# A trunk of retention, dilated attention and gated MLPs on one core: the denominators' selection issued later, a buffer of its own for the transposed values, and part of each layer end's norm work on VectorE

## The chip, the core and the metric

The kernel runs on one core of a Trainium2 chip. The metric is the device time of one execution in microseconds (us). A core has TensorE (PE in the profile, with its weight loads shown as PEld), VectorE (DVE), ScalarE (ACT), GpSimd (POOL) and SyncE (SP), which here only issues the DMAs. Each engine works through its own list of instructions in order and waits for the others on semaphores.

## What is computed

A decoder trunk of two layers over 512 tokens of width 1024, in float32. Layer 0 mixes by retention, layer 1 by dilated attention with three head groups; each is followed by a gated MLP. Every sub-layer is wrapped in two norms:

```
for layer in range(2):
    h = rmsnorm(x, norm_mix_pre[layer])
    m = retention_mixer(h, ...) if layer == 0 else dilated_mixer(h, w_q, w_o, k_sh, v_sh, pos)
    x = x + rmsnorm(m, norm_mix_post[layer])
    f = conv_ffn(rmsnorm(x, norm_ffn_pre[layer]), ...)
    x = x + rmsnorm(f, norm_ffn_post[layer])
    if layer == 0:
        k_sh, v_sh = shared_kv(x, kv_norm, att_w_kv, pos)
```

In the attention the outputs of the three groups of a head are merged by their softmax denominators, which comes to one common maximum and one common sum over the three groups:

```
outs, lses = [], []
for gi, (window, dilation) in enumerate(((128, 1), (512, 4), (2048, 16))):
    o, l = dilated_group_attention(q[:, :, gi], k_sh[:, :, gi], v_sh[:, :, gi], window, dilation)
alpha = softmax(stack(lses), axis=0)
o = einsum('gbsh,gbshd->bshd', alpha, stack(outs))
```

## The kernel before

**Stages.** The program is unrolled: retention (to about 400 us of the profile), first MLP (to 795 us), attention (to 1357 us), second MLP. The 512 tokens are four blocks of 128 rows (`NB` = 4). Each product of two float32 matrices is made of three matmuls (`mm3`, L208 to L210) on a high and a low part of each operand. A weight tile comes by DMA into `raw` (3 buffers), is multiplied by a gain on GpSimd in the attention (L158), and is parted into `whi` on ScalarE (L168) and `wlo` on VectorE (L169).

**Layer ends (`finish`, `prenorm`).** In the last output projection of a sub-layer `contract` goes over the blocks b and, in each, over two halves c of the width. After a half, `after(b, c)` runs: VectorE has added the half to `m` (L271), ScalarE sums its squares (`squares`, L221), and `m` is multiplied with the post-norm's row into `h` (L323). After the second half `rms` makes v_rms (L225) and `rstd` r_rms (L215) on GpSimd; the block's generator then adds to the residual x (L305, VectorE). `prenorm` follows for the next sub-layer: squares of x in two halves, v_rms and r_rms, the scaled rows `h` (L256, or L254 where there is no gain row), four transposes a half on TensorE (L264), and their parting into `hT_hi` (L198) and `hT_lo` (L199). The order on VectorE and GpSimd is as written here (`manual_schedule(engines=ORD)`); TensorE's and ScalarE's order is made by the scheduler that builds the program. In the next MLP `up_first` does its products for tokens 0 to 255 of four weight units, and the last two blocks' steps are called from inside it. At the program's end the last half's product is on VectorE already (`end`).

**Attention (`heads`).** Heads are worked in eight pairs hp. While `heads` does the scores, softmax and output of pair hp, `_weave` interleaves it with a generator `fill` that makes the keys, queries and values of pair hp+1: at each `yield` of `heads` two to four steps of `fill` (three matmuls each) are put in. There the order on TensorE is as written (`manual_schedule(engines={E.PE})`), those of VectorE and ScalarE are the scheduler's, and all are fixed when the program is built.

- `residue_values` makes the values of the dilated groups: the product in `pm`, a copy `vT` to SBUF on ScalarE (L674), and four transposes on TensorE some steps later (L693). `vT` is allocated under the tag `sh`, of which there is one buffer.
- `rotated` makes keys and queries: VectorE shuffles `pm` into `sh` (L714) and multiplies `pm` into `m` (L716, L720), GpSimd multiplies `sh` (L717, L721) and adds it to `m` (L718, L722). `sh` is that same one buffer.
- The scores `sc` (L756) of groups 1 and 2 read four such `m`; VectorE masks them (L760).
- `weights` transposes the probabilities in eight pieces i = 0 to 7 (L846) into `pt`, copied to `pT` by VectorE for even i (L852) and by ScalarE for odd i (L850). `apply` multiplies them with the values into `po` (L866).
- `select` spreads the denominators over a matrix on VectorE (L778) and multiplies with it on TensorE into `pz` (L785); `gather` picks the result up on VectorE (L790, L795), whose inverse (L882, L883) is spread by ScalarE (L885) and transposed (L895) for the last product (L896). `pt`, `pz` and part of `sc` share the PSUM tag `tr`, with two buffers.

Of the kernel before, what the change touches and what calls it, by code (L numbers as in the profile page):

```python
# [17 lines left out]
P = 128  # L18
# [78 lines left out]
def trunk(ctx: ExitStack, tc: tile.TileContext, a, out):  # L97
# [132 lines left out]
    def prenorm(b, gain, both=False):  # L230

        ss = small.tile([P, 2], F32, name="ss", tag="ss")
        for c in range(2):
            if both and c == 1:
                junk = norm.tile([P, 512], F32, name="h", tag="h", bufs=HB)
                nc.vector.tensor_tensor_reduce(
                    out=junk,
                    in0=x[b][:, half(c)],
                    in1=x[b][:, half(c)],
                    scale=1.0 / D,  # L240
                    scalar=0.0,
                    op0=ALU.mult,
                    op1=ALU.add,
                    accum_out=ss[:, c : c + 1],
                )
            else:
                squares(x[b], ss, c)
        r = rms(ss)
        yield
        hs = []  # L250
        for c in range(2):
            h = norm.tile([P, 512], F32, name="h", tag="h", bufs=HB)
            if gain is None:
                nc.vector.tensor_scalar(out=h, in0=x[b][:, half(c)], scalar1=r, scalar2=None, op0=ALU.mult)  # L254
            else:
                nc.vector.scalar_tensor_tensor(  # L256
                    out=h, in0=x[b][:, half(c)], scalar=r, in1=gain[c], op0=ALU.mult, op1=ALU.mult
                )
            hs.append(h)
        yield  # L260
        for c in range(2):
            pt = ps.tile([P, 4, P], F32, name="pt", tag="tr")
            for j in range(4):
                nc.tensor.transpose(out=pt[:, j, :], in_=hs[c][:, blk(j)], identity=ident)  # L264
            split(pt, hi[:, c * 4 : c * 4 + 4, blk(b)], lo[:, c * 4 : c * 4 + 4, blk(b)])
# [27 lines left out]
    def finish(left, w, row, then, ahead=(), tag="po", early=None):  # L293
# [21 lines left out]
        def after(b, c):  # L315
            if c == 0:
                ss[b] = small.tile([P, 2], F32, name="ss", tag="ss")
                steps[b], mg[b] = block(b), []
            mg[b].append(norm.tile([P, 512], F32, name="h", tag="h", bufs=HB))
            squares(m[b], ss[b], c)  # L320
            end = then is None and b == NB - 1
            eng = nc.vector if end and c == 1 else nc.gpsimd
            eng.tensor_mul(out=mg[b][c], in0=m[b][:, half(c)], in1=gain[:, half(c)])  # L323
            if early and ahead:
                t = 2 * b + c
                if t in EP:
                    units.append(parts(raws[len(units)]))
            if c == 0:
                if b >= 1:
                    next(steps[b - 1], None)  # L330
                if b >= 2:
                    next(steps[b - 2], None)
            else:
                rs[b] = rms(ss[b], nc.vector if end else nc.gpsimd)
                if ahead and not early and b == 1:
                    units.append(parts(raws[0]))
                if ahead and not early and b == F4:
                    raws.append(fetch(*ahead[3]))
                if ahead and not early and b == 3:
                    units.append(parts(raws[1]))  # L340
                if b >= 1:
                    next(steps[b - 1], None)
# [270 lines left out]
    def attention(pool, post, then, late, ahead):  # L613
# [11 lines left out]
        with pool as tmp:  # L625
# [37 lines left out]
            def residue_values(hp, g, res):  # L663
# [4 lines left out]
                for k in range(KT):  # L668
                    mm3(pm, [t[:, blk(k)] for t in wu], (hi[:, k, :], lo[:, k, :]), k == 0, k == KT - 1)
                    aged(k)  # L670
                    if k < KT - 1:
                        yield
                vT = tmp.tile([P, SEQ], F32, name="vT", tag="sh", bufs=1)
                nc.scalar.copy(out=in_runs(vT), in_=by_residue(pm))  # L674
                v = rtiles[hp % 2 * 2 + g - 1]
                pending.append([vT, v, 0])
# [54 lines left out]
            def heads(hp, ks, qs, vs, vr, res):  # L731
# [102 lines left out]
                def weights(i, rb):  # L834
# [9 lines left out]
                    for h in range(2):  # L844
                        for n, p in enumerate(src):
                            nc.tensor.transpose(out=pt[:, h, n, :], in_=p[:, h, :], identity=ident)  # L846
                    pT = tmp.tile([P, 2, 2, P], F32, name="pT", tag="pT", bufs=6)
                    n = len(src)
                    if i % 2:
                        nc.scalar.copy(out=pT[:, :, 0:n, :], in_=pt[:, :, 0:n, :])  # L850
# [19 lines left out]
                for i in range(0, 8, 2):  # L870
# [1 line left out]
                        for t in prev:  # L872
                            apply(*t)
                    prev += [(j, order[j], *weights(j, order[j])) for j in (i, i + 1)]
                    if i == 2:
                        pz = select(den[:, 8:16], quarter, sel[:, 0:128])
                    yield
                    yield

                inv = small.tile([P, 8], F32, name="inv", tag="inv", bufs=2)  # L880
                gather(pz, residue, inv)
                nc.vector.tensor_add(out=inv, in0=inv, in1=den[:, 0:8])  # L882
                nc.vector.reciprocal(out=inv, in_=inv)  # L883
                spread = tmp.tile([P, 2, 2, P], F32, name="pT", tag="pT", bufs=6).rearrange("p a b q -> p (a b q)")
                nc.scalar.copy(  # L885
                    out=spread.rearrange("p (c d) -> p c d", d=HD), in_=inv.unsqueeze(2).broadcast_to([P, 8, HD])
                )
# [68 lines left out]
    def pre(row):  # L956
        g = []

        def run(b):
            if not g:  # L960
                t = gain_rows(row)
                g.extend(t[:, half(c)] for c in range(2))
            return prenorm(b, g)

        return run

    mix, ffn_ = a["norm_mix_post"], a["norm_ffn_post"]
    late = retention(pool("ret", "left"), mix[0], pre(a["norm_ffn_pre"][0]), ffn_first(0))
    late = ffn(0, pool("ffn0", "right"), ffn_[0], lambda b: prenorm(b, None), late, att_first())
    late = attention(pool("att", "left"), mix[1], pre(a["norm_ffn_pre"][1]), late, ffn_first(1))  # L970
    ffn(1, pool("ffn1", "right"), ffn_[1], None, late)

# [42 lines left out]
```

## Time and profile before

| | |
|---|---|
| median of 3 runs | 1747.56 us (1743.99 to 1750.20) |
| the profiled execution | 1750.31 us |
| its span, first to last instruction | 1748.5 us |
| mean granted TensorE clock | 0.991 of full speed |
| PE busy in the span | 98% |
| DVE, ACT, POOL busy | 54%, 35%, 23% |
| PE's idle between its own first and last instruction, gaps of over 0.06 us | 28.9 us in 19 places |

The profile has a page of totals, a list of who waited for whom (in total, times, longest), a timeline in which every row has start, duration, engine, line and operation, and in brackets the engine's idle time just before it with what ended that; and busy times by stretch with the clock that the throttle granted. `pz L785 <- DVE pT L852` reads: the instruction of line 785 that writes `pz` stood idle until the instruction of line 852 that writes `pT` on VectorE was done. A matmul's end is modelled, so that a shown idle time of PE starts where the model ends the matmul before.

### The profile page before, as it was taken

To read this page: it belongs to the slowest core of one execution; us is meant where nothing else is said; L and a number is where in the kernel's file an instruction comes from. 1 tells how busy PE (TensorE), PEld (TensorE's weight loads), DVE (VectorE), ACT (ScalarE), POOL (GpSimd) and SP (SyncE) were. 2 spreads that over 40 slices of the span, in tenths; PEclk is the share of its full clock that TensorE was granted. 3 is DMA by queue.
4 is the path that set the end of the run, shared out by engine and by line. 5 is a ranking of instruction groups with operands and counts; after the bars stand their busy time and mean duration, and the time that the engine had idled before them with its cause. 6 is when DMAs were issued, how large, how long until landed. Compare 5 with 4: busy or idle time off the path is not lost.

```text
span 1748.5 us, 21650 instructions
## 1 busy us (share of the span) xinstructions
PE 1709.0 (98%) x8590; PEld 1417.3 (81%) x8590; DVE 939.2 (54%) x1461; ACT 613.3 (35%) x1076; POOL 397.5 (23%) x284
## 2 busy tenths in 40 slices
PE   9999999999999999999899999999999999999998
PEld 6888888887888888878778888878887788888886
DVE  4553545468544544557546556556455754454454
ACT  5232422325442422423144243244245544233241
POOL 1000000005000000046665656566431400000003
PEclk9999999999999999999999999999999999999999
DMA  6422333214332332432222222222221333233231
GB/s 211 125 67 84 91 97 91 85 36 109 121 96 73 121 96 73 133 106 61 85 71 64 85 73 81 68 70 85 69 73 44 87 116 97 83 111 96 84 109 49
DMA packets 202162, 156.10 MB, mean 89 GB/s; under 512 B 4989, under 2 KB 182093, under 8 KB 202062
## 3 DMA queue, kind: packets, MB, share of 16 engines
q1 hardware_dynamic: 202062, 154.73, 28.9%
q8 instruction: 67, 1.10, 0.3%
q14 instruction: 33, 0.27, 0.0%
HBM read 152.62 MB, written 2.10 MB: 88 GB/s over the span
## 4 chain that ended last, share of the span: by engine, by line
PE 89%; DVE 5%; POOL 3%; ACT 1%; issue 1%; DMA 1%; POOLq 0%; SPq 0%; DVEq 0%; ACTq 0%
PE pm L208 20%; PE pm L210 20%; PE pm L209 20%; PE po L208 6%; PE po L209 6%; PE po L210 6%; PE sc L756 2%; DVE wlo L169 2%; PE po L866 2%; PE pt L846 1%; DVE x L305 1%; PE s L450 1%; PE pt L264 1%; DVE h L256 1%; POOL raw L158 1%
## 5 line engine op out<-in xcount | busy, mean ns | idle before, releaser
L208 PE MATMUL pm<-hT_hi,whi 128*128 128x512 f32 (+1 forms) x1424 | 546.3, 384 | 0.0
L209 PE MATMUL pm<-hT_lo,whi 128*128 128x512 f32 (+1 forms) x1424 | 540.0, 379 | 0.3 <-DVE hT_lo L199 0.3
L210 PE MATMUL pm<-hT_hi,wlo 128*128 128x512 f32 (+1 forms) x1424 | 539.7, 379 | 0.0
L169 DVE TENSOR_TENSOR wlo<-raw,whi 128x1024 fp32r<-128x1024 f32 x275 | 377.7, 1378 | 299.9 <-ACT whi L168 296.2
L168 ACT CAST whi<-raw 128x1024 fp32r<-128x1024 f32 x275 | 286.0, 1051 | 650.0 <-PE pm L209 355.3
L208 PEld LDWEIGHTS pm<-hT_hi,whi 128*128 128x128 f32 x1424 | 269.6, 189 | 51.5 <-issue 3.2
L210 PEld LDWEIGHTS pm<-hT_hi,wlo 128*128 128x128 f32 x1424 | 269.3, 189 | 50.1
L209 PEld LDWEIGHTS pm<-hT_lo,whi 128*128 128x128 f32 x1424 | 269.6, 189 | 48.5 <-DVE hT_lo L199 1.2
L158 POOL TENSOR_TENSOR raw<-raw,cols 128x1024 f32<-128x1024 f32 x72 | 140.7, 1957 | 465.8 <-DMA raw<-in_att_w_kv 385.6
L271 DVE TENSOR_TENSOR m<-po,m 128x512 f32<-128x512 f32 x112 | 77.1, 688 | 139.0 <-PE po L210 138.8
L208 PE MATMUL pm<-whi,hT_hi 128*128 128x512 f32 (+1 forms) x384 | 142.2, 370 | 0.0
L323 POOL TENSOR_TENSOR h<-m,gain 128x512 f32<-128x512 f32 x31 | 47.4, 1528 | 407.7 <-DVE m L271 407.2
L208 PE MATMUL po<-whi,ah 128*128 128x512 f32 x352 | 137.9, 392 | 0.0
L209 PE MATMUL po<-wlo,ah 128*128 128x512 f32 x352 | 137.9, 392 | 0.0
L210 PE MATMUL po<-whi,al 128*128 128x512 f32 x352 | 137.8, 391 | 0.0
L210 PE MATMUL pm<-whi,hT_lo 128*128 128x512 f32 (+1 forms) x384 | 136.9, 356 | 0.0
L209 PE MATMUL pm<-wlo,hT_hi 128*128 128x512 f32 (+1 forms) x384 | 136.7, 356 | 0.0
L215 POOL TENSOR_TENSOR r_gn<-v_gn,nhalf 128x1 f32<-128x1 f32 x16 | 8.8, 548 | 357.4 <-DVE v_gn L480 357.4
L208 PEld LDWEIGHTS pm<-whi,hT_hi 128*128 128x128 f32 x384 | 73.0, 190 | 11.5 <-issue 1.0
L209 PEld LDWEIGHTS pm<-wlo,hT_hi 128*128 128x128 f32 x384 | 73.1, 190 | 10.8 <-DVE wlo L169 0.6
L210 PEld LDWEIGHTS pm<-whi,hT_lo 128*128 128x128 f32 x384 | 72.8, 190 | 10.7 <-DVE hT_lo L199 0.3
L208 PEld LDWEIGHTS po<-whi,ah 128*128 128x128 f32 x352 | 66.5, 189 | 14.2 <-DVE m L271 0.4
(137 smaller groups left out, 1959.8 us busy)
## 6 DMA issues: line engine op xcount, KB each, us to landing
raw<-in_ffn_w_up SPq DMA_DIRECT2D x88, 512.0 KB, 3.8
raw<-in_att_w_kv SPq DMA_DIRECT2D x48, 512.0 KB, 4.0
raw<-in_ret_w_in SPq DMA_DIRECT2D x47, 512.0 KB, 3.9
raw<-in_ffn_w_down SPq DMA_DIRECT2D x44, 512.0 KB, 3.2
raw<-in_att_w_q SPq DMA_DIRECT2D x24, 512.0 KB, 3.7
raw<-in_ret_w_out SPq DMA_DIRECT2D x16, 512.0 KB, 3.3
raw<-in_att_w_o SPq DMA_DIRECT2D x8, 512.0 KB, 3.3
x<-in_x SPq DMA_DIRECT2D x3, 512.0 KB, 6.6
```

Of the source, the lines that this page charges most:

```text
L158: nc.gpsimd.tensor_mul(out=dst, in0=dst, in1=gain.unsqueeze(2).broadcast_to(list(src.shape)))
L168: nc.scalar.copy(out=hi, in_=raw)
L169: nc.vector.tensor_sub(out=lo, in0=raw, in1=hi.bitcast(F32))
L208: nc.tensor.matmul(o, lhsT=l[0], rhs=r[0], start=start, stop=False)
L209: nc.tensor.matmul(o, lhsT=l[0], rhs=r[1], start=False, stop=False)
L210: nc.tensor.matmul(o, lhsT=l[1], rhs=r[0], start=False, stop=stop)
L256: nc.vector.scalar_tensor_tensor(out=h, in0=x[b][:, half(c)], scalar=r, in1=gain[c], op0=ALU.mult, op1=ALU.mult)
L264: nc.tensor.transpose(out=pt[:, j, :], in_=hs[c][:, blk(j)], identity=ident)
L271: nc.vector.tensor_add(out=dst, in0=src, in1=dst)
L323: eng.tensor_mul(out=mg[b][c], in0=m[b][:, half(c)], in1=gain[:, half(c)])
L756: nc.tensor.matmul(pm[h][:, i, c], lhsT=q, rhs=k, start=True, stop=True)
L866: nc.tensor.matmul(dst, lhsT=v, rhs=p, start=i == 0 and g == 0, stop=i == 7)
```

## The change

Four things are edited.

1. In `heads`, the `select` of the denominators is issued after the transposes of pieces 4 and 5 and one `yield`, instead of directly behind those of pieces 2 and 3.
2. `vT` has a tag of its own, and so a buffer of its own. `pT` has five buffers instead of six.
3. At every layer end, not only at the program's, the product of the last block's second half with the norm's row is on VectorE instead of GpSimd. (v_rms and r_rms stay on GpSimd except at the program's end.)
4. In the `prenorm` of the last block at the three inner layer ends, the squares of the second half of x are summed by VectorE (L236) instead of ScalarE; its unused product goes to a small tile `junk2` instead of an `h` buffer.

```
@@ prenorm
             if both and c == 1:
-                junk = norm.tile([P, 512], F32, name="h", tag="h", bufs=HB)
+                junk = norm.tile([P, 512], BF16, name="junk2", tag="junk2", bufs=1)
                 nc.vector.tensor_tensor_reduce(
@@ finish, after(b, c)
-            end = then is None and b == NB - 1
+            end = b == NB - 1
             eng = nc.vector if end and c == 1 else nc.gpsimd
             eng.tensor_mul(out=mg[b][c], in0=m[b][:, half(c)], in1=gain[:, half(c)])
...
-                rs[b] = rms(ss[b], nc.vector if end else nc.gpsimd)
+                rs[b] = rms(ss[b], nc.vector if end and then is None else nc.gpsimd)
@@ residue_values
-                vT = tmp.tile([P, SEQ], F32, name="vT", tag="sh", bufs=1)
+                vT = tmp.tile([P, SEQ], F32, name="vT", tag="vT", bufs=1)
@@ heads, weights
-                    pT = tmp.tile([P, 2, 2, P], F32, name="pT", tag="pT", bufs=6)
+                    pT = tmp.tile([P, 2, 2, P], F32, name="pT", tag="pT", bufs=5)
@@ heads
                     prev += [(j, order[j], *weights(j, order[j])) for j in (i, i + 1)]
-                    if i == 2:
+                    yield
+                    if i == 4:
                         pz = select(den[:, 8:16], quarter, sel[:, 0:128])
-                    yield
                     yield
...
-                spread = tmp.tile([P, 2, 2, P], F32, name="pT", tag="pT", bufs=6).rearrange("p a b q -> p (a b q)")
+                spread = tmp.tile([P, 2, 2, P], F32, name="pT", tag="pT", bufs=5).rearrange("p a b q -> p (a b q)")
@@ pre(row), and the same in the call of ffn(0, ...)
-            return prenorm(b, g)
+            return prenorm(b, g, b == NB - 1)
```

Three places show what this does to the order of instructions. The first is TensorE in the attention, head pair 0, around the selection (`pz`); rows are those of before with the change's + and -, and 38 rows lie between the two pieces.

```order
@@ -3840,5 +3842,4 @@
 L210 MATMUL pm<-hT_hi,wlo 128x512
 L846 MATMUL pt<-ident,p 128x128 x8
-L785 MATMUL pz<-spread,sel 128x32
 L208 MATMUL pm<-hT_hi,whi 128x512
 L209 MATMUL pm<-hT_lo,whi 128x512
@@ -3883,4 +3884,5 @@
 L209 MATMUL pm<-hT_lo,whi 128x512
 L210 MATMUL pm<-hT_hi,wlo 128x512
+L785 MATMUL pz<-spread,sel 128x32
 L208 MATMUL pm<-hT_hi,whi 128x512
```

The selection leaves its place directly behind eight transposes and now stands nine projection matmuls behind the transposes of pieces 4 and 5; 12, 18 or 9 matmuls follow before those of pieces 6 and 7 (pair 0, odd pairs, pairs 2, 4 and 6).

The second is VectorE in the attention, head pair 2 (pairs 4 and 6 are alike): the copies `pT` of pieces 4 and 6 and the pick-up of the selection (`z`, `inv`).

```order
 L169 TENSOR_TENSOR wlo<-raw,whi 128x1024
+L852 COPY pT<-pt 128x512
+L714 STREAM_SHUFFLE sh<-pm 128x512
+L716 TENSOR_TENSOR m_79<-pm,rope 128x512
+L169 TENSOR_TENSOR wlo<-raw,whi 128x1024
 L790 TENSOR_TENSOR z<-pz,sel 128x32
 L795 TENSOR_REDUCE inv<-z 128x8
 L882 TENSOR_TENSOR inv<-inv,den 128x8
 L883 RECIPROCAL inv<-inv 128x8
-L852 COPY pT<-pt 128x512
-L714 STREAM_SHUFFLE sh<-pm 128x512
-L716 TENSOR_TENSOR m_79<-pm,rope 128x512
```

The pick-up moves behind the copy of piece 4, a shuffle, a product and a `wlo`; in pairs 0, 1, 3 and 5 it stands directly behind the copy of piece 4. Nothing but these moves changes on VectorE within the attention, and ScalarE's order there is the same.

The third is VectorE at the end of the retention layer (the end of the attention is alike), with `x_76` the last block's residual and `m_80` its projection.

```order
 L271 TENSOR_TENSOR m_80<-po,m_80 128x512
+L323 TENSOR_TENSOR h<-m_80,gain 128x512
 L169 TENSOR_TENSOR wlo<-raw,whi 128x1024
 L256 SCALAR_TENSOR_TENSOR h<-x_75,r_rms,gain 128x512 x2
 L169 TENSOR_TENSOR wlo<-raw,whi 128x1024
 L305 SCALAR_TENSOR_TENSOR x_76<-h,r_rms,x_76 128x512 x2
-L199 TENSOR_TENSOR hT_lo<-pt,hT_hi 128x4x128 x2
+L199 TENSOR_TENSOR hT_lo<-pt,hT_hi 128x4x128
+L236 ISA junk_3268,ss<-x_76 128x512
+L236 ISA ss 128x1
+L199 TENSOR_TENSOR hT_lo<-pt,hT_hi 128x4x128
 L169 TENSOR_TENSOR wlo<-raw,whi 128x1024
```

The product and the squares are added; GpSimd loses the product and ScalarE one square. On TensorE the scheduler places the transposes of the last two blocks a little later at these two ends; in the `up_first` of the first MLP the eight of block 2 stood 36 matmuls behind those of block 1, and now stand 41 behind them:

```order
L209 MATMUL pm<-hT_lo,whi 128x256
L210 MATMUL pm<-hT_hi,wlo 128x256
L208 MATMUL pm<-hT_hi,whi 128x256
L209 MATMUL pm<-hT_lo,whi 128x256
L264 MATMUL pt<-ident,h 128x128 x4
L210 MATMUL pm<-hT_hi,wlo 128x256
L264 MATMUL pt<-ident,h 128x128 x4
L208 MATMUL pm<-hT_hi,whi 128x256
```

The eight of block 3 stood together 48 matmuls behind those of block 2; now they stand 47 behind the second four of block 2, and two matmuls lie between their own two fours. At the first MLP's end (into the attention) TensorE's order is unchanged.

More of the change, by code (lines that the diff above doesn't have):

```diff
@@ L968, in trunk @@
     late = retention(pool("ret", "left"), mix[0], pre(a["norm_ffn_pre"][0]), ffn_first(0))
-    late = ffn(0, pool("ffn0", "right"), ffn_[0], lambda b: prenorm(b, None), late, att_first())
+    late = ffn(0, pool("ffn0", "right"), ffn_[0], lambda b: prenorm(b, None, b == NB - 1), late, att_first())
     late = attention(pool("att", "left"), mix[1], pre(a["norm_ffn_pre"][1]), late, ffn_first(1))
```

## The prediction

> **What bounds the kernel now.** I read the totals first, then the list of waits for TensorE alone, and then the timeline around each wait.
>
> ```profile
> PE 1709.0 (98%) x8590; PEld 1417.3 (81%) x8590; DVE 939.2 (54%) x1461; ACT 613.3 (35%) x1076; POOL 397.5 (23%) x284
> ```
>
> TensorE is busy for 98% of the span. The change takes no matmul away, so it can gain only TensorE's idle time and its slow stretches. The waits:
>
> ```profile
> PE pt L264 <- DVE h L256: 9.9, 7, 2.0
> PE pz L785 <- DVE pT L852: 9.3, 7, 2.0
> PE pt L693 <- ACT vT L674: 5.0, 1, 5.0
> PE pt L264 <- DVE h L254: 4.4, 2, 3.0
> ```
>
> All four lines are touched by the diff: the second by the moved selection, the third by the buffer of `vT`, the others by the layer ends. Half of the `h` waits belong to blocks that the diff leaves alone.
>
> The second price of a wait is the clock (columns: stretch, its length, busy time of PE, PEld, DVE, ACT, POOL, granted clock, DMA):
>
> ```profile
> 896.00:899.70 3.70, 1.66 (x11) 1.29 (x10) 3.13 (x5) 0.58 (x1) 3.70 (x3) 1.00 0.21 54
> 899.70:903.10 3.40, 3.40 (x10) 2.62 (x9) 1.39 (x2) 0.00 (x0) 3.40 (x3) 0.50 0.37 112
> 1097.60:1101.00 3.40, 3.10 (x15) 2.60 (x16) 1.79 (x5) 0.00 (x0) 2.06 (x2) 1.00 0.54 154
> 1227.40:1230.80 3.40, 3.40 (x10) 2.63 (x10) 1.53 (x4) 0.00 (x0) 1.95 (x3) 0.50 0.53 154
> 858.70:865.60 6.90, 5.18 (x37) 4.63 (x38) 3.91 (x10) 1.17 (x2) 2.94 (x2) 0.51 0.49 142
> 428.70:432.10 3.40, 3.40 (x17) 3.40 (x18) 3.40 (x5) 2.11 (x5) 0.84 (x1) 0.50 0.88 242
> ```
>
> After some waits the clock stands at 0.50 for 3.4 us (once for twice that). At half speed 3.4 us do 1.7 us of work, so such a stretch costs 1.7. After the equally long wait near 1097.9 the clock stayed at 1.00, so not every 2-us wait sets it off. The stretches lie on a grid of 3.41 us.
>
> [...]
>
> **The selection.** Columns are start, duration, engine, line, and in brackets the idle time just before with what ended it.
>
> ```profile
> 895.23 0.39 PE L210 MATMUL pm<-hT_hi,wlo 128*128 128x512 f32 x1
> 895.46 1.04 PE L846 MATMUL pt<-ident,p 128*128 128x128 f32 x8
> 895.99 1.89 DVE L169 TENSOR_TENSOR wlo<-raw,whi 128x1024 fp32r<-128x1024 f32 x1 [0.56 <-ACT whi L168]
> 897.80 0.68 DVE L852 COPY pT<-pt 128x512 f32<-128x512 f32 x1
> 898.53 0.41 PE L785 MATMUL pz<-spread,sel 128*128 128x32 f32 x2 [2.04 <-DVE pT L852]
> 898.98 0.19 DVE L790 TENSOR_TENSOR z<-pz,sel 128x32 f32<-128x32 f32 x1 [0.50 <-PE pz L785]
> ```
>
> `pz` stands directly behind the eight transposes and takes the PSUM buffer of the first four. VectorE empties that buffer at 897.80, and only behind a `wlo` that began first. So TensorE stands still for 2.04. Moved, nine matmuls stand between: starts are 0.23 apart (895.23 to 895.46), so 2.1 us of work covers VectorE's copy. The places where `pz` will stand, and where its result will be picked up:
>
> ```profile
> 908.65 0.69 DVE L852 COPY pT<-pt 128x512 f32<-128x512 f32 x1 [1.25 <-PE pt L846]
> 912.59 0.01 DVE L714 LOAD_MASK_SELECT sh<-pm  x1 [3.25 <-PE pm L210]
> 1036.35 1.54 POOL L722 TENSOR_TENSOR m<-m,sh 128x512 f32<-128x512 f32 x1
> 1040.00 0.01 DVE L714 LOAD_MASK_SELECT sh<-pm  x1 [0.51 <-PE pm L210]
> 1041.25 1.97 DVE L169 TENSOR_TENSOR wlo<-raw,whi 128x1024 fp32r<-128x1024 f32 x1
> 1043.15 0.82 PE L846 MATMUL pt<-ident,p 128*128 128x128 f32 x6
> ```
>
> The copy of piece 4 (908.65) runs as soon as its transposes are there; VectorE waited 1.25 for them. It is done 0.7 later, inside the 2.1. In pairs 0, 1, 3 and 5 VectorE then stands at `z` until `pz` comes; queued behind is a shuffle that now waits 3.25 for TensorE, so this costs nothing. In pairs 2, 4 and 6 `z` stands behind shuffle, product and `wlo`, which ends at 1043.22; with 0.19 for `z`, its buffer is free at 1043.4. The transposes that need it come four behind 1043.15, plus 0.14 for `pz`: about 1043.7. The margin is 0.3. If this cover fails, TensorE waits by what is lacking.
>
> So 9.3 of waiting go. A matmul's end is modelled some 0.15 late, so each shown gap is that much short: +1.0 for seven. In pair 7 no projections are left, `pz` has one matmul of cover, and I take off 0.3. Gain 10.0 (bounds: 0 if the wait comes back at piece 7; 10.3). The two half-clock stretches behind these waits (899.7, 1227.4) go with them: 2 x 1.7 = 3.4 (bounds 0 to 3.4). Five `pT` buffers instead of six make the copy of piece 5 take that of piece 0, whose `apply` is issued earlier in the same order: nothing. If it were not, a copy would wait for one `apply`.
>
> **The buffer of `vT`.**
>
> ```profile
> 853.29 1.06 ACT L168 CAST whi<-raw 128x1024 fp32r<-128x1024 f32 x1 [6.36 <-PE pm L209]
> 857.64 0.41 DVE L760 CUSTOM_DVE_ANT_0 p<-sc,mask 128x256 f32<-128x256 f32 x1
> 858.23 1.51 POOL L722 TENSOR_TENSOR m<-m,sh 128x512 f32<-128x512 f32 x1
> 859.78 0.58 ACT L674 COPY vT<-pm 128x512 f32<-128x512 f32 x1 [5.43 <-POOL m L722]
> 860.41 1.11 PE L693 MATMUL pt<-ident,vT 128*128 128x128 f32 x4 [4.96 <-ACT vT L674]
> 861.46 1.23 PE L756 MATMUL sc<-m 64*128 64x128 f32 x8
> ```
>
> The copy on ScalarE waits for GpSimd's last read of the shared buffer (858.23 + 1.51 = 859.74). With its own it can start at 853.29 + 1.06 = 854.35, and the transposes have no wait. But the eight score products behind them (861.46) read the `m` that the same GpSimd addition writes at 859.74, and no buffer changes that. They began 1.7 after it and can begin right after it: the gain is 861.46 - 859.74 = 1.7, not 5.0. TensorE then stands about 3.3 at the scores instead of 5.0 at the transposes. The 6.9 us of half clock behind (858.7) may shrink to one stretch or not: 0 to 1.7, I take 0.8. This chain on GpSimd begins at the layer end, so what the layer end gains moves it as well.
>
> **The layer ends.**
>
> ```profile
> 424.66 1.21 DVE L169 TENSOR_TENSOR wlo<-raw,whi 128x1024 fp32r<-128x1024 f32 x1
> 424.75 1.28 POOL L225 TENSOR_SCALAR v_rms<-ss 128x1 f32<-128x1 f32 x1 [3.03 <-ACT junk L221]
> 426.64 1.27 POOL L323 TENSOR_TENSOR h<-m,gain 128x512 f32<-128x512 f32 x1
> 426.71 2.42 DVE L256 SCALAR_TENSOR_TENSOR h<-x,r_rms,gain 128x512 f32<-128x512 f32 x2 [0.84 <-POOL r_rms L215]
> 797.88 0.30 POOL L225 TENSOR_SCALAR v_rms<-ss 128x1 f32<-128x1 f32 x1 [1.46 <-ACT junk L221]
> 798.84 1.29 POOL L323 TENSOR_TENSOR h<-m,gain 128x512 f32<-128x512 f32 x1
> 800.23 0.63 POOL L225 TENSOR_SCALAR v_rms<-ss 128x1 f32<-128x1 f32 x1
> 809.23 0.41 PE L264 MATMUL pt<-ident,h 128*128 128x128 f32 x2 [1.41 <-DVE h L254]
> L323 DVE TENSOR_TENSOR h<-m,gain 128x512 f32<-128x512 f32 x1 | 0.7, 691 | 0.0
> L236 DVE CUSTOM_DVE_ANT_0 h<-x 128x512 f32<-128x512 f32 x1 | 0.7, 693 | 4.6 <-DMA x<-in_x 4.6
> ```
>
> The last two rows price the added work where VectorE already does it: 0.69 each for product and squares, three times each, 4.1 in all on an engine that is 54% busy. GpSimd loses three products of 1.3. Whether GpSimd or VectorE runs, the other is held: v_rms takes 1.28 beside a `wlo` and 0.30 alone, and two `h` rows take 2.42 beside GpSimd's product.
>
> Into the first MLP, the `h` rows that TensorE waits 2.0 for (block 2) run free of that product, while 0.69 is put ahead of them on VectorE: I take 0.5 earlier (bounds -0.7 to +1.0). TensorE does five products more before it needs them, 0.12 each (half of 0.23, being half as wide): 0.6. With 1.1 of 2.0 gone its half-clock stretch (428.7) goes too, 1.7. Block 3's `h` comes after the added squares and gives 0.7 back. Together 2.1. Into the attention, v_rms (800.23) no longer stands behind the product that starts at 798.84, so the second half of block 3 comes 0.7 to 0.9 earlier, against a wait of 1.41: 0.9. Into the second MLP, no half clock followed: 0.4 + 0.6 = 1.0. Sum 4.0 (bounds -2 to 5). No DMA is moved on any queue.
>
> [...]
>
> **Sum.** 10.0 + 3.4 + 1.7 + 0.8 + 4.0 = 19.9, from the profiled execution's 1750.31: 1730.4. That execution lies 2.75 above the median of the three, about what one or two half-clock stretches cost; a run with fewer of these has less to lose of them, so I expect the same end for the median: 1730.
>
> **Rivals.**
> - *The half clock comes anyway.* The grid is fixed, the waits that remain may fall into it differently. For it: 2.03 at 1097.9 had none. Then 3.4 and the 0.8 do not come: about 1735. Chance 0.19.
> - *GpSimd does not hold the scores.* If its chain moves forward when `vT` is out of its way, the wait near 860 goes wholly: 3.3 more, 1727. Against it: GpSimd's additions stand behind each other with no wait for `vT`. Chance 0.10.
> - *VectorE and GpSimd hold each other at the layer ends.* v_rms is blocked by the new product or squares; the ends give 0: 1734. Chance 0.14.
> - *The selection's wait returns at piece 7.* The margin of 0.3 fails in pairs 2, 4, 6, and pair 7 has no cover: two thirds of the 13.4 stay or less, 1735 to 1739. Chance 0.06.
> - *Slower than before.* `z` now stands behind the shuffle `sh`, and that one waits for GpSimd where its single buffer is not free:
>
> ```profile
> DVE sh L714 <- POOL m L722: 11.4, 3, 5.8
> ```
>
>   Were that so at the new place, TensorE would stand at piece 7 for up to 5.8 in each of eight pairs: 46, and 1777. It decides once GpSimd's addition (1036.35 + 1.54 = 1037.9) ends more than 2.1 later, behind the shuffle's 1040.0. Nothing that the diff moves delays it by that. Chance 0.02.
>
> **How the numbers follow.** The sum as it stands has 0.45; 0.04 is left for no change that can be told. 0.3%, or 5 us, is about what a measurement of this kernel can tell from no change. All but the last rival and that rest end under 1742: faster 0.93, same 0.04, slower 0.03. The range goes down to 1723 (`vT` wholly, the ends at their bound, the clock at its best) and up to 1738 (no clock gain and half of the ends). The sum's own range is 1727 to 1734.
>
> **What would show it.** Right: no wait of `pz` on `pT` in the list; `vT`'s wait replaced by one of some 3 us of `sc` on `m L722`; full clock at 899 and 1227; `h L256` at about 6 instead of 9.9. Wrong: a wait of `pt L846` on `z L790`, a new wait of `pz`, v_rms of over 1 us at the layer ends, or half-clock stretches in new places.

## The result, and the profile after

The changed kernel takes 1731.17 us (median of six runs, 1728.70 to 1732.50) against 1746.38 us of the kernel before (six runs, 1742.76 to 1750.20): a ratio of 0.9911 with a 95% interval of 0.9894 to 0.9928, 15.2 us less. The forecast was 1730 in a range of 1723 to 1738. The profiled execution took 1732.50 (span 1730.7, clock 0.995).

The list of waits of TensorE in the changed kernel, in total, times and longest:

```profile
PE 1703.0 (98%) x8590; PEld 1412.4 (82%) x8590; DVE 934.5 (54%) x1470; ACT 612.1 (35%) x1070; POOL 396.8 (23%) x281
...
PE pt L264 <- DVE h L256: 7.9, 8, 2.0
PE pt L264 <- DVE h L254: 4.8, 3, 3.0
PE sc L756 <- POOL sh L721: 2.3, 1, 2.3
PE po L517 <- DMA gain<-in_norm_mix_pre: 2.2, 1, 2.2
PE sc L756 <- POOL m L722: 1.1, 1, 1.1
PE pm L209 <- DVE hT_lo L199: 0.8, 3, 0.3
PE pt L693 <- DVE mst L760: 0.6, 1, 0.6
```

The 9.3 us of `pz` are gone. The 5.0 us at `vT` have become 2.3 + 1.1 at the scores and 0.6 at the transposes. On the first page line TensorE's busy time falls by 6 us with the same 8590 matmuls: that is fewer matmuls at half clock (0.50 for eight times 3.41 us before, four times now, without the stretch at the program's end). TensorE's gaps of over 0.06 us add up to 17.8 us, from 28.9.

The place of the selection in head pair 2 of the changed kernel (timeline):

```profile
1031.04 0.30 PE L785 MATMUL pz<-spread,sel 128*128 128x32 f32 x2
1033.17 0.18 DVE L790 TENSOR_TENSOR z<-pz,sel 128x32 f32<-128x32 f32 x1
1033.33 0.82 PE L846 MATMUL pt<-ident,p 128*128 128x128 f32 x6
```

`pz` has no bracket: it waited for nothing. `z` is done at 1033.35. The transposes that need its buffer come behind four others, so about half a microsecond after 1033.33 (four of 0.14 each); the narrow margin of the prediction held in all pairs.

Busy time by stretch with the granted clock (the column behind POOL's) shows what remains of the half clock:

```profile
408.80:412.20 3.40, 1.37 (x10) 0.89 (x9) 2.78 (x3) 0.29 (x1) 3.19 (x4) 1.00 0.52 154
412.20:415.60 3.40, 3.40 (x12) 2.72 (x10) 3.40 (x5) 2.84 (x8) 1.71 (x2) 0.50 0.00 0
...
852.50:855.90 3.40, 0.67 (x6) 0.33 (x4) 3.40 (x10) 0.59 (x1) 3.32 (x3) 1.00 0.25 66
855.90:859.30 3.40, 2.76 (x26) 2.76 (x28) 2.75 (x8) 0.00 (x0) 2.16 (x2) 0.50 0.45 134
859.30:862.80 3.50, 3.50 (x13) 2.70 (x12) 3.22 (x13) 0.00 (x0) 1.72 (x2) 0.51 0.38 112
...
1344.00:1347.40 3.40, 1.37 (x8) 0.78 (x7) 2.56 (x4) 0.05 (x1) 3.14 (x5) 1.00 0.55 154
1347.40:1350.90 3.50, 3.50 (x12) 2.91 (x12) 3.50 (x5) 2.93 (x8) 1.95 (x2) 0.51 0.00 0
```

The stretches at 428.7, 899.7 and 1227.4 have no counterpart. The one at the scores is still twice 3.4 us. One before the attention went (783.64 before, twice 3.4 us) and one behind it came (1347.44 now), at waits that the change does not touch.

**Where the time went, by one method.** The same matmul is looked up in both traces; the difference of its starts is the gain up to there. The first row of each pair is of the kernel before, the second of the changed kernel:

```profile
809.61 0.36 PE L208 MATMUL pm<-whi,hT_hi 128*128 128x256 f32 x1
...
866.84 0.39 PE L208 MATMUL pm<-hT_hi,whi 128*128 128x512 f32 x1
...
1291.78 0.48 PE L208 MATMUL pm<-hT_hi,whi 128*128 128x512 f32 x1
```

```profile
805.57 0.36 PE L208 MATMUL pm<-whi,hT_hi 128*128 128x256 f32 x1
...
862.55 0.49 PE L208 MATMUL pm<-hT_hi,whi 128*128 128x512 f32 x1
...
1273.19 0.48 PE L208 MATMUL pm<-hT_hi,whi 128*128 128x512 f32 x1
```

Up to the attention 4.04 us are gained, up to the end of the first scores 4.29, and behind the seventh selection 18.59. Taken like this at every step (us):

| step | predicted | found |
|---|---|---|
| selection, without its clock | 10.0 | 11.1 - 0.4 in pair 7 = 10.7 |
| its two half-clock stretches | 3.4 | 3.2 |
| buffer of `vT`, with clock | 2.5 | 0.25 |
| first layer end, with clock | 2.1 | 2.1 |
| second layer end | 0.9 | 0.4 |
| third layer end | 1.0 | 0.7 |
| half clock and waits elsewhere | 0 | +1.6 at 783, -1.4 at 1347 |
| sum | 19.9 | 17.5 |

Between the two profiled executions lie 17.8 us; the rest is at the program's start and end. The table compares one execution of each kernel, and the experiments show how much of it changes from one execution to the next.

### The profile page after: what moved, and what is told of

The parts are those of the page before. It is cut to its first block, busy times and chain, and to the rows that moved or that the text cites. A ratio compares the mean times of both kernels' runs of the same rounds, so it can differ in the third digit from the quotient of the medians.

```text
span 1730.7 us, 21655 instructions
## 1 busy us (share of the span) xinstructions
PE 1703.0 (98%) x8590; PEld 1412.4 (82%) x8590; DVE 934.5 (54%) x1470; ACT 612.1 (35%) x1070; POOL 396.8 (23%) x281
## 4 chain that ended last, share of the span: by engine, by line
PE 91%; POOL 3%; DVE 3%; DMA 1%; issue 1%; ACT 1%; POOLq 0%; SPq 0%; DVEq 0%; ACTq 0%
PE pm L208 21%; PE pm L210 21%; PE pm L209 21%; PE po L208 6%; PE po L209 6%; PE po L210 6%; PE sc L756 2%; PE po L866 2%; PE pt L846 2%; DVE x L305 1%; PE s L450 1%; POOL r_rms L215 1%; POOL h L323 1%; DVE wlo L169 1%; PE pt L264 1%
## 5 line engine op out<-in xcount | busy, mean ns | idle before, releaser
L169 DVE TENSOR_TENSOR wlo<-raw,whi 128x1024 fp32r<-128x1024 f32 x275 | 371.5, 1356 | 297.0 <-ACT whi L168 293.5
L158 POOL TENSOR_TENSOR raw<-raw,cols 128x1024 f32<-128x1024 f32 x72 | 145.1, 2017 | 455.2 <-DMA raw<-in_att_w_kv 373.2
L323 POOL TENSOR_TENSOR h<-m,gain 128x512 f32<-128x512 f32 x28 | 41.9, 1496 | 405.5 <-DVE m L271 405.2
L208 PEld LDWEIGHTS pm<-whi,hT_hi 128*128 128x128 f32 x384 | 73.0, 190 | 11.6 <-issue 1.0
```

Source lines behind the costliest of these rows:

```text
L158: nc.gpsimd.tensor_mul(out=dst, in0=dst, in1=gain.unsqueeze(2).broadcast_to(list(src.shape)))
L169: nc.vector.tensor_sub(out=lo, in0=raw, in1=hi.bitcast(F32))
L208: nc.tensor.matmul(o, lhsT=l[0], rhs=r[0], start=start, stop=False)
```

## The experiments

The selection, the buffer of `vT` and the two edits at the layer ends together were each run alone first, and of these two the product alone; the squares were not run alone. Times are medians; the gain is against the kernel before in the same job, whose median was between 1744.9 and 1747.1.

**The selection alone.**

```
-                    if i == 2:
+                    yield
+                    if i == 4:
                         pz = select(den[:, 8:16], quarter, sel[:, 0:128])
-                    yield
                     yield
```

> The kernel before with the later selection alone (six pT buffers, vT on the shared buffer). Theory (the waits of pz and the half-clock stretches behind them are most of the gain): the seven waits of pz on pT (9.3 us) are gone from the list, no wait of the transposes on z appears, and the time is 10 to 14 us under the kernel before, about 1734 us. Rival (most of the gain is the clock's luck in the runs compared): the waits go, but the time falls by under 8 us, to 1739 us or more. In either case the vT wait near 860 stays at about 5 us.

Measured: 1733.64 against 1744.93 us, ratio 0.9942 (0.9926 to 0.9959), 11.3 us less. No wait of `pz` and none on `z` is in the list, and `vT` waits as before. The theory holds: this edit is three quarters of the gain.

**The buffer of `vT` alone** (tag `vT`, five `pT` buffers).

> The kernel before with a buffer of its own for vT and five pT buffers. Theory (GpSimd's chain of products and additions for the first head pair's keys and queries bounds the scores): the wait of 5 us at vT turns into waits of the scores on GpSimd of 3 to 4 us in sum, the half-clock stretch there stays and now covers work, and the time is within 0 to 2 us of the kernel before. Rival (the shared buffer was the bound): no wait of over 1 us is left at that place and the time falls by 4 to 6 us, to about 1741 us.

Measured: 1744.07 us, ratio 0.9993 (0.9981 to 1.0004): no gain that can be told. Its waits of TensorE:

```profile
PE pz L785 <- DVE pT L852: 6.0, 7, 2.1
...
PE sc L756 <- POOL sh L721: 2.4, 1, 2.4
...
PE sc L756 <- POOL m L722: 1.1, 1, 1.1
...
PE pt L693 <- DVE mst L760: 0.4, 1, 0.4
```

The wait of 5.0 became 3.9 in three pieces under new names. The theory holds, the rival falls. The first line shows something else: the waits of `pz` are 6.0 here, and 6.2 in the next two kernels, where the profile of before had 9.3. In pairs 3 and 5 the wait is 0.35 in these three and was 2.03 in that one execution. So that profile was an unfavourable one for the selection. These three kernels also have one half-clock stretch at a selection (near 895), where it had two.

**The layer ends alone** (product and squares), and **the product alone**.

```
-            end = then is None and b == NB - 1
+            end = b == NB - 1
...
-            return prenorm(b, g)
+            return prenorm(b, g, b == NB - 1)
```

(The small tile `junk2` and the engine of v_rms go with them as in the change; the product alone has the first of the two lines, and v_rms as in the change.)

> The kernel before with the layer-end edits alone (second half's product and squares of the last block on VectorE). Theory: at the first layer end the wait of TensorE on h falls from 2.0 to about 0.7 and the half clock behind it goes; at the second it falls from 1.4 to 1.0; at the third from 1.1 to about 1.0 in two pieces: 2 to 4 us in sum, about 1743.5 us. Rival (VectorE and GpSimd hold each other): the waits on h keep their sum of about 14 us, v_rms takes over 1 us at each of the ends, and the time stays within 1 us of the kernel before.

> The kernel before with the product of the last block's second half on VectorE, the squares left on ScalarE. Theory (the product is what held VectorE's h rows of block 2, the squares only bring block 3 forward): the first and third ends gain as with both edits, and at the second end the wait on h of block 3 stays near 1.4: 1 to 3 us, about 1744.5 us. Rival (the squares carry the gain): this kernel stays within 1 us of the kernel before while both edits together gain 2 or more.

Measured: 1742.97 us with both, ratio 0.9992 (0.9980 to 1.0003), and 1744.51 us with the product alone, 0.9998 (0.9985 to 1.0012). Neither can be told from no change by its time. The waits can be read. First the kernel with both edits, then the one with the product alone:

```profile
PE pt L264 <- DVE h L256: 7.7, 8, 2.0
...
PE pt L264 <- DVE h L254: 3.9, 2, 3.0
```

```profile
PE pt L264 <- DVE h L256: 9.4, 8, 2.0
...
PE pt L264 <- DVE h L254: 4.3, 2, 3.0
```

Together they were 14.3 before, are 13.7 with the product and 11.6 with both. By place: the product brings block 2's wait at the first end from 2.00 to 0.68; block 3 then waits 0.99, which the squares lower to 0.36; at the second end the wait of 1.41 stays at 1.37 with the product and falls to 0.89 with the squares (block 2's and block 3's waits at the first end are those of the kernel with the product and of the changed kernel, where the blocks ahead of them stand alike). So each edit does what it should at its own block, for 2.7 us of waits in sum. That the squares take more off the sum than the product was not in the theory of the second run, which gave them the second end only.

The first end needs a caution. The kernel with the selection alone leaves this end as it was, and TensorE yet waits differently there:

```profile
418.61 1.29 PE L264 MATMUL pt<-ident,h 128*128 128x128 f32 x8 [0.87 <-DVE h L256]
426.87 0.63 PE L264 MATMUL pt<-ident,h 128*128 128x128 f32 x4 [1.10 <-DVE h L256]
```

These are 0.87 at block 1 and 1.10 at block 2 in place of 2.00 at block 2, with no half clock behind. By the same matmul this execution gains 2.8 us on the profile of before at this end, without any edit to it. The kernel with both edits at the layer ends shows this second course too, with 0.86, 0.14 and 0.36. Like with like, the edits take 0.6 to 0.9 us off the waits at this end. The clock differs here too: behind the 2.00 at block 2 the profile of before has 0.50 for 3.41 us (from 428.66), and that of the changed kernel, behind its 0.68, has 1.00. What decides between the two courses is not shown.

**Cover or place?** The selection was moved to a place behind other matmuls and to one where VectorE is free. Both runs start from the kernel before. The first keeps the place and gets the cover (the `yield`), the second moves the place without cover.

```
+                    yield
                     if i == 2:
                         pz = select(den[:, 8:16], quarter, sel[:, 0:128])
-                    yield
                     yield
```

```
-                    if i == 2:
+                    if i == 4:
                         pz = select(den[:, 8:16], quarter, sel[:, 0:128])
```

> The kernel before with the selection after the transposes of pieces 2 and 3 as there, but behind one yield, so that nine to twelve projection matmuls stand between (2.1 us or more). Theory (the cover is what counts: VectorE's wlo and copy take 1.89 + 0.68 us, and are done about when nine matmuls are): the waits of pz on pT sum to under 1 us, and the time is within 2 us of the kernel with the later selection alone, about 1734 us. Rival (the place counts, since at the old one VectorE is behind with a wlo): 3 us or more of these waits stay, and the time is 1738 us or more.

> The kernel before with the selection directly behind the transposes of pieces 4 and 5, without the yield between. Theory (without cover pz waits for one copy of 0.69 us that begins after four of the eight transposes): each wait is about 0.35 us as in those pairs of the kernel before where no wlo was in front, 2.5 us in sum, no half clock follows, and the time is about 1736 us. Rival (the place alone takes the waits away, as VectorE is idle there): under 0.7 us in sum and about 1734 us; or a wlo in front there too: 6 us and over, about 1743 us.

Measured: 1735.11 us with the cover, ratio 0.9940 (0.9918 to 0.9963), and no wait of `pz` in its list; 1741.15 us with the place alone, ratio 0.9975 (0.9960 to 0.9990), and this line:

```profile
PE pz L785 <- DVE pT L852: 3.1, 7, 1.1
```

Six of the seven waits are 0.35. The cover alone gives the whole gain, 11.5 us; a place without cover about half. The waits came as expected (3.1 for 2.5), the time 5 us later than expected. About half of that is the price of a shown wait: from the first to the seventh selection this kernel falls 5.1 us behind the kernel with the later selection, for 3.1 us of shown waits, about 0.6 for each 0.35, where 2.5 was expected; by their medians the two are 5.8 apart in gain. The waits of before say the same: 0.35 cost 0.62, 0.95 cost 1.20, 2.03 cost 2.25. A shown wait of TensorE is about 0.25 us short. Another 1.7 is that the kernel before was itself slower in this job (1746.63, after 1744.93 in the first).

**What holds the scores near 855?** The changed kernel's rows there:

```profile
842.43 0.73 DVE L714 STREAM_SHUFFLE sh<-pm 128x512 f32<-128x512 f32 x1
...
849.45 0.01 DVE L714 LOAD_MASK_SELECT sh<-pm  x1 [2.81 <-POOL m L722]
...
850.79 1.90 POOL L158 TENSOR_TENSOR raw<-raw,cols 128x1024 f32<-128x1024 f32 x1 [1.38 <-DMA raw<-in_att_w_kv]
852.64 2.24 POOL L721 TENSOR_TENSOR sh<-sh,rope 128x512 f32<-128x512 f32 x1
854.97 1.52 POOL L722 TENSOR_TENSOR m<-m,sh 128x512 f32<-128x512 f32 x1
...
854.94 0.49 PE L756 MATMUL sc<-m 64*128 64x128 f32 x4 [2.26 <-POOL sh L721]
856.54 2.72 PE L756 MATMUL sc<-m 64*128 64x128 f32 x22 [1.10 <-POOL m L722]
```

The scores wait for GpSimd's product and addition. First that last rotation was given to VectorE:

```
-                _run(rotated(w_q, g * D, g_q, kq[0][1]))
+                _run(rotated(w_q, g * D, g_q, kq[0][1], eng=nc.vector if g == 2 else nc.gpsimd))
```

(`eng` does the product of the shuffled half and the addition.)

> The changed kernel with the last rotation of head pair 0 (group 2's queries: product of the shuffled half and addition) on VectorE instead of GpSimd. Theory (GpSimd's chain bounds the scores there, which is why the buffer for vT gave so little): the waits of the scores on GpSimd (3.4 us in sum) fall to under 1.5 us, the half clock there gets shorter, and the time is 2 to 5 us under the changed kernel, 1726 to 1729 us. Rival (VectorE's own list or the weights' transfers bound the scores): a wait of 2.5 us or more stays there under another name, and the time is within 1.5 us of 1731 us.

Measured: 1731.23 us, ratio 0.9919 (0.9896 to 0.9941), no better than the changed kernel. Its line:

```profile
PE pt L693 <- DVE mst L760: 4.1, 1, 4.1
```

The rival holds: the wait came back whole, now on VectorE's masks `mst`, which free the PSUM buffer. Both engines stand in one ring. VectorE's shuffle waits 2.81 (6.13 at the first) for GpSimd's addition to free the one `sh`; behind the shuffle stand `wlo` and the masks; `wlo` frees the `raw` buffer, and GpSimd's next `raw` waits 1.38 for the transfer into it. From one shuffle to the next it is 7.0 us (842.43 to 849.45), for 24 matmuls of 0.23, 5.5 us. The next kernel opens the ring and leaves the order on every engine as it is:

```
-                u = tmp.tile([P, SEQ], F32, name="sh", tag="sh", bufs=1)
+                u = tmp.tile([P, SEQ], F32, name="sh", tag="pT" if own else "sh", bufs=5 if own else 1)
...
-                _run(rotated(w_kv, g * D, g_kv, kq[0][0]))
+                _run(rotated(w_kv, g * D, g_kv, kq[0][0], own=True))
```

(and the same for the queries).

> The changed kernel in which the four rotations of head pair 0 built ahead of the loop (keys and queries of groups 1 and 2) write their shuffled half into the pT buffers, idle then, instead of the single sh buffer; every engine's order is the same. Theory (the single sh buffer ties VectorE and GpSimd into a ring of about 7 us a rotation against 5.5 us of matmuls: the shuffle waits 2.8 to 6.1 us for GpSimd's addition, and the masks of the scores and the next transfer stand behind it): the waits of the shuffle for GpSimd go there, the 4.0 us that TensorE waits at the scores near 855 fall to under 1 us, the half clock there goes, and the time is 3 to 7 us under the changed kernel: 1724 to 1728 us. Rival (GpSimd's 5.7 us of work for each rotation and the transfers in front of it bound the scores by themselves): 2.5 us or more of waits stay at the scores and the time is within 1.5 us of 1731 us.

Measured: 1728.62 us against 1747.13, ratio 0.9894 (0.9873 to 0.9916). Its waits:

```profile
DVE sh L714 <- POOL m L722: 3.9, 1, 3.9
...
PE sc L756 <- POOL m L722: 2.7, 1, 2.7
```

The gain of 18.5 us is 3.3 more than that of the changed kernel, with overlapping intervals. The first line was 15.7 in four waits there; the wait that is left, at 896, is in the loop, where `sh` keeps its one buffer. The ring is gone and the half clock at the scores is one stretch instead of two, but 2.7 of the 4.0 us stay: GpSimd now works without a gap there, 5.7 us a rotation (1.90 + 2.25 + 1.52) instead of one every 7.0. Each explanation had part of it: the ring set the pace, and just behind it GpSimd's own work does.

**The rows of block 3 at the first MLP's end.** In the changed kernel VectorE makes them here:

```profile
795.95 0.88 DVE L254 TENSOR_SCALAR h<-x,r_rms 128x512 f32<-128x512 f32 x2
...
800.82 5.98 POOL L158 TENSOR_TENSOR raw<-raw,cols 128x1024 f32<-128x1024 f32 x3
...
800.89 4.15 DVE L254 TENSOR_SCALAR h<-x,r_rms 128x512 f32<-128x512 f32 x2
```

The same two rows take 0.88 us for one block and 4.15 for another, beside GpSimd's products of `raw`. In the kernel before they took 3.51 there. Each of the two ends 0.28 after a product does (803.00 after 802.72, 805.04 after 804.76).

```
-                nc.vector.tensor_scalar(out=h, in0=x[b][:, half(c)], scalar1=r, scalar2=None, op0=ALU.mult)
+                nc.scalar.activation(h, x[b][:, half(c)], AF.Copy, scale=r) if b == NB - 1 else nc.vector.tensor_scalar(...)
```

> The changed kernel with the two h rows of block 3 at the first MLP's end (L254) on ScalarE instead of VectorE. Theory (there VectorE is held by GpSimd's three products of raw, which begin at the same moment: 4.15 us for two rows against 0.88 us without them): the two take 1.2 to 1.5 us on ScalarE, the wait of TensorE there (0.95 us) goes, and the time falls by 0.5 to 2 us, to about 1730 us. Rival (ScalarE is as late, or the chain behind takes it back at the scores): the wait stays or comes back near 855, within 0.5 us of 1731 us.

> The changed kernel with both edits: the rotations of head pair 0 through the pT buffers, and the two h rows of block 3 at the first MLP's end on ScalarE. Theory (the two waits are apart): the gains add, 4 to 8 us under the changed kernel, about 1724 us. Rival (the earlier rows only move the wait at the scores): no better than the better of the two alone by more than 0.5 us.

Measured: 1726.59 us with this edit alone, ratio 0.9888 (0.9867 to 0.9910), and 1724.83 us with it and the opened ring, 0.9871 (0.9847 to 0.9896). On ScalarE the two rows take 1.34:

```profile
800.15 1.34 ACT L254 ACTIVATE h<-x,r_rms 128x512 f32<-128x512 f32 x2 [0.77 <-POOL r_rms L215]
```

TensorE's wait there is gone (block 3's `h` at the second end: 0.95 in the changed kernel, none here), and so the theory holds; its expected 0.5 to 2 us came as 1.1 us less idle time in the profiles (gaps of 16.7 for 17.8). By the medians against the kernel before in each job it is 5.3 us more than the changed kernel gained, but the intervals overlap, and this kernel's granted clock is 0.996 to 0.998 in its runs where the changed kernel's is 0.994 to 0.998: the rest is half clock in the profiles (TensorE busy 2.4 us less), and how much of it the edit causes stays open. With both edits the wait at the scores is 1.1 us, since GpSimd's chain also begins earlier. This kernel is 22.3 us under the kernel before, and its interval overlaps that of the changed kernel only from 0.9894 to 0.9896: the version to keep.

**Block 0.** The squares of block 0's second half on VectorE as well.

```
-            return prenorm(b, g, b == NB - 1)
+            return prenorm(b, g, b in (0, NB - 1))
```

> The changed kernel with the squares of block 0's second half on VectorE too at the three inner layer ends. Theory (the two squares in turn on ScalarE are on the path of h; splitting them shortens it by about half a us, as at block 3): the waits of TensorE on h of block 0 (2.0, 3.0 and 2.0 us) fall by 0.3 to 0.7 us each, 1 to 2 us in sum, and half-clock stretches behind them may go: 1728 to 1730 us. Rival (VectorE's order gives it back to the next block): the waits of block 0 fall and others rise by as much, and the time stays within 1 us of 1731 us.

Measured: 1732.39 us, ratio 0.9922 (0.9901 to 0.9943): no gain. At the second end the wait of block 0 fell from 2.96 to 1.87, but TensorE waits 0.70 there for a sum of another block, and at the other two ends block 0's wait rose from 2.03 to 2.38. The rival holds.

**`vT` back on the shared buffer**, the rest of the change kept.

> The changed kernel with vT back on the single sh buffer and six pT buffers: the selection and the layer ends alone. Theory (in the closed ring the own buffer moves the wait from vT to the scores and is worth about 1 us of idle time): the wait at vT is 5 us or more again, no wait stands at the scores, and the time is 0 to 2 us over the changed kernel. Rival (the own buffer carries a part of the gain of its own): 3 us or more over it, 1734 us and up.

Measured: 1731.91 us, ratio 0.9922 (0.9902 to 0.9942), with 14.4 us of gain in its job against the 15.2 of the changed kernel. Its wait at `vT`:

```profile
PE pt L693 <- ACT vT L674: 6.0, 1, 6.0
```

By the same matmuls ahead of `vT` and behind the scores, the own buffer is worth 1.0 us in this pair of profiles. The theory holds.

## Why the prediction was right, and where it was not

The time was right: 1731.2 measured for 1730 forecast. The single terms were less right than the sum, and part of the fit is luck.

- *What bounds.* Right. TensorE's list of waits named the four places, and each edit alone changed the line it was expected to.
- *The selection* (10.0 + 3.4 forecast, 13.9 found in the traces). The step held, and the run with the cover alone shows its mechanism: nine matmuls cover the copy and the `wlo`. Mis-sized was the correction for the modelled end of a matmul: 0.15 a wait was taken, 0.25 is what the same matmul shows. It went the other way in the usual run: the three kernels that left the selection in place had 6.0 to 6.2 of these waits, not 9.3, and the selection alone is worth 11.3 us there. The sum from one profile was 19.9; the medians moved by 15.2. The forecast of 1730 still fits, since a gain 4.7 too large was taken from a profile 3.9 above the median of before. The prediction had foreseen for the clock, but not for the waits, that a slower profile has more to lose; that the two nearly cancel is luck.
- *The buffer of `vT`* (1.7 + 0.8 forecast, 0.25 found). The scores do begin right behind the addition (856.54 after 856.49), and "not 5.0, since the scores wait for GpSimd's addition" was right, as the run with this edit alone shows. The step that failed is that the gain would be the whole 1.7. It took the addition on GpSimd to move with TensorE. TensorE came 4.0 us earlier, the addition 3.25 (859.74 to 856.49), so 4.0 us of waits stay for 3.3 forecast. The edit is not what delays the addition. Counted from the last transpose of `h` ahead of the attention, it ended after 50.2 us in the profile of before and 51.0 in that of the changed kernel; but over the seven kernels with the shared buffer this lies between 50.2 and 51.2, and over the four with the own buffer and an unchanged ring between 50.1 and 51.0. The profile of before was the earliest of its seven, and what spreads these times is not shown. That the ring sets the pace, the run that opens it shows. Nor did the half clock shrink: the two slow windows now hold 2.76 + 3.50 us of work at half speed, before 5.18, and the 1.1 more cost half of that. Three waits in place of one, each shown about 0.25 short, take back the rest. With this edit alone there is one slow window instead of two, and 1.5 us are found at this place. So the term is 0.3 to 1.5 by the execution, not 2.5.
- *The layer ends* (2.1 + 0.9 + 1.0 forecast, 2.1 + 0.4 + 0.7 found). At the first end the mechanism was right: the two `h` rows took 1.42 without GpSimd's product beside them instead of 2.42, and the half clock behind went. That the size fits is luck in part: like with like the edits are worth 0.6 to 0.9 us of waits, and the 1.7 of half clock only in executions that had it; the selection alone shows 2.8 at this end without them.

```profile
424.87 0.81 POOL L225 TENSOR_SCALAR v_rms<-ss 128x1 f32<-128x1 f32 x1 [3.02 <-ACT junk L221]
...
425.51 1.21 DVE L169 TENSOR_TENSOR wlo<-raw,whi 128x1024 fp32r<-128x1024 f32 x1
427.18 1.42 DVE L256 SCALAR_TENSOR_TENSOR h<-x,r_rms,gain 128x512 f32<-128x512 f32 x2 [0.45 <-POOL r_rms L215]
```

v_rms is still held by VectorE (0.81 beside the new product, 1.28 before beside the `wlo`), so the third rival had its mechanism, not its price. At the second end the rows of block 3 began 1.1 earlier against TensorE, as forecast, but took 4.15 beside GpSimd's products instead of 3.51, which the term missed; the rows quoted for it showed only v_rms. At the third end the waits went from 1.92 (0.81 at block 1 and 1.11 at block 2) to 1.38 in four pieces (0.07, 0.67 and 0.35 at blocks 1 to 3, and 0.29 at a matmul between).
- *The clock.* The two stretches behind `pz` went as said. The first rival came true elsewhere, both ways: -1.4 at a wait of 2.03 that is the same in both kernels, +1.6 at another.
- *Slower than before.* No wait of the transposes on `z` anywhere.
- *The signs.* The waits of `pz` went and the scores wait for GpSimd, as said. `h L256` fell to 7.9, not to about 6, and one half-clock stretch stands in a new place (1347.4), which was named as a sign of being wrong: it is the first rival, in part.
- *Slips that changed little.* Of the 14.3 us of `h` waits, 4.5 were at blocks 2 and 3 of the inner ends, which the edits reach: two thirds, not half, belong to other blocks. The margin at piece 7 comes to 0.4 by the prediction's own rows (four transposes of 0.14, and `pz`). The chances listed give 0.94 faster and 0.02 slower, not 0.93 and 0.03.

## What to carry to other kernels

A matmul that needs the buffer just filled in front of it wants other matmuls in between, as many as the emptying engine's copy plus one instruction that may have begun before it; here these took 0.68 and 1.89 us, nine matmuls 0.23 apart were enough (no wait of `pz` was left), and where they stand mattered little (11.5 us gained at the old place, 11.3 at the new). When a buffer of its own takes a wait away, look for the next reader of the same chain before counting the wait as gain: here a single buffer, two engines and a transfer formed a ring, and the edit that opened the ring took the wait from 4.0 to 2.7 us. Size a term that rests on one execution by several, if some of its waits can take two values.

## What the runs showed of the hardware

**Where the clock stood at half.** Ahead of the program's end the profile of before has six stretches at 0.50, four of 3.41 us and two of 6.83 (from 783.64 and 858.74); that of the changed kernel has three, two of 3.41 and one of 6.83 (from 855.93). In each of the two profiles their starts lie whole multiples of 3.413 us apart (411.59 and 1227.38 before by 239 of them). In the 3.41 us ahead of these nine stretches TensorE was busy for 0.13 to 1.66 us. Two others on the same grid with no more work in them were followed by 1.00: 1.61 busy from 1094.25 on before, and 1.46 from 780.83 on in the changed kernel. In the six short stretches TensorE was busy throughout; in the first 3.41 us of the three long ones it was busy for 2.20, 1.74 and 2.80. The two at the scores, both 6.83 us long, begin inside a wait, of 4.96 before and of 1.10 in the changed kernel. The length of a wait alone does not tell whether 1.7 us more are lost: the 2.03 at block 0 of the third end had no half clock behind it before (it ended at 1364.81) and had one in the changed kernel (1346.66, the stretch from 1347.44). What decides it is not shown.

Most of the spread of the times goes with the clock. Over 29 runs of the kernel before in one job the time rises by 1.6 us for each 0.001 that the mean clock falls. Of these runs the fastest took 1741.19 us at a mean clock of 0.996, the slowest 1751.17 at 0.990. A stretch of 3.41 us at half speed lowers the mean by 0.001 and costs 1.7 us; six of them are 10.2, and the two runs lie 9.98 apart.

**VectorE beside GpSimd.** Two scaled rows (`tensor_scalar`) took 0.88 us where no product ran on GpSimd (795.95) and 4.15 beside its products of `raw`, each row ending 0.28 behind a product. The products began first (800.82, the rows 800.89). By what a product holds a row, no run shows. Moving them to ScalarE, at 1.34 us, took TensorE's wait of 0.95 away.
